# Half of a kernel's intermediate stores moved from the SP queue to the GpSimd queue

## The chip, the core and the metric

The kernel runs on one core of one Trainium2 chip. The metric is the device time of one execution in microseconds (us), and the number for a kernel is the median over several runs. A core has five engines that run side by side: TensorE (PE in the profile; its weight loads are the row PEld), VectorE (DVE), ScalarE (ACT), GpSimd (POOL) and SyncE (SP). Transfers are issued by an engine's instruction stream, in the order in which the instructions stand, and carried out by 16 DMA engines that all streams share.

## The reference

```python
"x": np.random.randn(16, 512, 768), "w1": (768, 3072), "b1": (3072,), "w2": (3072, 768)   # all float32
y = np.matmul(x, w1) + b1
y = 0.5 * y * (1.0 + erf(y / np.sqrt(2.0)))
return np.matmul(y, w2).astype(np.float32)
```

A two-layer perceptron with an exact GELU between the layers: 8192 rows, 768 inputs, 3072 hidden values, 768 outputs.

## The kernel before, in words

Everything is multiplied in fp16 with fp32 sums. Both products go through a bilinear scheme with 20 block products in place of 24: operands are sums and differences of tiles that DVE forms (L341), PE multiplies them, and DVE and ACT combine the partial results from PSUM into the outputs.

**Phase 1** makes g = gelu(x w1 + b1), transposed. The first 512 rows of x are multiplied plainly. The other rows are six blocks, `BLK`: block 0 and block 1 have three pieces of 256 rows each, blocks 2 to 5 three pieces of 512. A block runs through units (three units when pieces have 256 rows, six when they have 512); a unit has 20 products of three or six matmuls (L853) and yields 12 finished tiles of g. For each finished tile, `finish` (L531) adds one ACT instruction with GELU (L537; two for 256-row pieces) that writes a slot of `gst`, a ring of 13 slots of 128 x 512 fp16, and one DMA (L542) that stores the slot, 128 KB, to the tensor `gd` in HBM. A GELU whose slot has not yet been stored must wait. There are 384 such stores: 24 plain ones, 36 in block 0, 36 in block 1 and 72 in each of the blocks 2 to 5.

**Where x comes from.** `x_cast1` (L673) issues from GpSimd a DMA that converts 256 rows of x to fp16 into the tensor `xd` in HBM (L677). `load_x` (L718) issues from SP a transposing DMA from `xd` into one of two x buffers (L728), during the block before the one that uses it. Casts stand one block ahead of the transposes.

**GpSimd's gates.** GpSimd computes nothing in phase 1 after the start. So that a cast does not start too early, `marker` (L377) has DVE write one element after a given product, and `gated` (L368) has GpSimd copy that element (L372) before it issues the DMA. A gated DMA, and all that stands behind it in GpSimd's stream, waits for that copy. In block 4 the gated DMAs are twelve casts of w2 into HBM (L894); in block 5 GpSimd loads w2 and the first g tiles (L934, L988).

**Phase 2** loads g back from `gd`, three 1 MB transfers for each 512 rows (L988), multiplies with w2 (L1026), and stores the outputs from SP (L1049).

**The order** is neither the compiler's nor written out by hand. `Sched` holds tasks with the engines that may run them and planned durations, for example `{"SP": 0.45}` for a store. `S.add` appends a task; `run` (L174) plays the plan forward in model time and emits the task that can start first, with due times for those that prepare later work. PE's tasks keep their written order. So a changed planned duration or engine can also move other tasks in their streams.

Of the kernel before, what the change touches and what calls it, by code (L numbers as in the profile page):

```python
# [252 lines left out]
def kernel(  # L253
# [8 lines left out]
    nc = tc.nc  # L262
# [36 lines left out]
    def a16(off, n):  # L299
        return ar[:, off // 2: off // 2 + n]  # L300
# [4 lines left out]
    S = Sched()  # L305
# [20 lines left out]
    def act_ps(n, src=0):  # L326
        return (n * 0.734 + 267 + src) / 1000
# [33 lines left out]
    def w1_ap(u, w, kt):  # L361

        return a16(O_W1 + (u // 2 * 20 + w) * 2 * W1T + kt * 512 + u % 2 * 256, P)
# [163 lines left out]
    gdone = [[] for _ in range(NU)]  # L527
    stores = []
    gvals = []

    def finish(src, t, row, n, sg, frees):  # L531

        g = Val(gst)
        k = 512 // n
        ft = []
        for y in range(k):
            ft.append(S.add({"ACT": act_ps(n)}, lambda e, y=y: nc.scalar.activation(  # L537
                out=a16(O_GST + g.slot * 1024 + y * n * 2, n), in_=src[1]()[:, y * n:(y + 1) * n], func=ACTF.Gelu,
                bias=b1t[:, t + y:t + y + 1], scale=float(sg)), reads=src[0], frees=frees,
                alloc=g if y == 0 else None, makes=[g], after=ft))  # L540
        un, c0 = row // 512, row % 512
        stores.append(S.add({"SP": 0.45}, lambda e: nc.sync.dma_start(  # L542
            out=gd[un][:, t:t + k, c0:c0 + n], in_=a16(O_GST + g.slot * 1024, 512).rearrange("p (t r) -> p t r", r=n)),
            reads=[g], nbytes=P * 512 * 2, bulk=2))
        gdone[un].append(stores[-1])
        gvals.append(g)
        return ft[-1]
# [117 lines left out]
    BLK = [((512, 768, 1024), 256), ((1280, 7680, 7936), 256)]  # L665
# [68 lines left out]
    def plain_pair(p):  # L734
        for i in range(0, 8, 2):
            qu = [(j // 2, 2 * p + j % 2) if p == 0 else (j % 4, 2 * p + j // 4) for j in (i, i + 1)]
            bv = [Val(bank), Val(bank)]
            for h in range(2):
                for (q, u), b in zip(qu, bv):
                    def mm(e, q=q, u=u, b=b, h=h):  # L740
                        for kc in range(3 * h, 3 * h + 3):
                            nc.tensor.matmul(out=ps[:, b.slot, :],  # L742
                                             lhsT=a16(O_WS[u // 2] + q * 3072 + kc * 512 + u % 2 * 256, P),
                                             rhs=a16(O_XT0 + kc * 1024, 512), start=(kc == 0), stop=(kc == KC - 1),
                                             skip_group_check=True)
                    w = whalf[q][h] if p == 0 else wparts[u][q]
                    t = S.add({"PE": 3 * 0.2158}, mm, reads=[w, x0T], frees=[wsv[u // 2], x0h],
                              **(dict(makes=[b]) if h else dict(alloc=b, makes=[])), after=plain_mm[-1:])
                    if h:
                        plain_mm.append(t)  # L750
            for (q, u), b in zip(qu, bv):
                finish(([b], lambda b=b: ps[:, b.slot, :]), q * 6 + u, 0, 512, 1, [b])
# [3 lines left out]
    def x1_transposes():  # L756
        for s in range(6):
            j, c = divmod(s, 2)
            tr_nat.append(transpose_tile(x1n[s], lambda kc, s=s: a16(O_XN + 6144 + s * 1536 + kc * 256, P),
                                         lambda j=j, c=c: x_third(0, j)[:, :, c * P:(c + 1) * P], xsv[0][j]))  # L760
            xsv[0][3 + j].prods = xsv[0][j].prods
# [30 lines left out]
    def x_sums(b, due0, dur):  # L792

        n = BLK[b][1]
        val = {i: (xsv[b][i], lambda i=i, b=b: xs_ap(b, i)) for i in range(6)}
        outs = {}
        for w, (i, sg) in enumerate(P1_XOUT):
            outs[i] = w
            assert sg == 1
        firstuse = {}  # L800
        for i, (c, w, xx) in enumerate(P1F_ORD):
            firstuse.setdefault(xx, i)
        need = {}
        for (d, op, a, z) in reversed(P1_XOPS):
            need[d] = min(need.get(d, 99), firstuse[outs[d]] if d in outs else 99)
            for q in (a, z):
                need[q] = min(need.get(q, 99), need[d])
        prev = []
        for (d, op, a, z) in sorted(P1_XOPS, key=lambda o: need[o[0]]):
            assert op != "N"  # L810
            va, fa = val[a]
            vb, fb = val[z]
            v = Val({0: sum_first, 1: sum_second, len(BLK) - 1: sum_last}.get(b, sumpool))
            due = due0 + dur * need[d]

            prev = [S.add({"DVE": dve_tt(3 * n)}, lambda e, fa=fa, fb=fb, v=v, op=op: comb(
                e, a16(v.slot, 3 * n), op, fa(), fb()), reads=[va, vb], alloc=v, order=prev, due=due, lock=True)]
            val[d] = (v, lambda v=v: a16(v.slot, 3 * n))
        return [val[i] for (i, sg) in P1_XOUT]
# [8 lines left out]

    def p1_block(b):
        r0, n = BLK[b]  # L830
        dur = 3 * (512 // n) * (n / 2.4 + 2.5) / 1000
        if b:
            xo = x_sums(b, S.pe_ideal, dur)
        last = []
        prods.clear()
        nst = len(stores)
        npair = 512 // n
        for u in range(0, 6, npair):
            if b == 0:
                plain_pair(u // 2)  # L840
                if u == 0:
                    x1_transposes()
                    xo = x_sums(b, S.pe_ideal, dur)
                w1_ops(u // 2, S.pe_ideal - 1.0, ([], w1cast, tr_nat + x0cast)[u // 2], dur)

            ORD, OPS = (P1F_ORD, P1F_OPS) if u == 0 else (P1_ORD, P1_OPS)

            def mm(bk, i, first, lst, u=u, ORD=ORD):
                c, w, xx = ORD[i]
                xa = xo[xx][1]()  # L850
                for kt in range(3):
                    for y in range(npair):
                        nc.tensor.matmul(out=ps[:, bk, y * n:(y + 1) * n],  # L853
                                         lhsT=w1_ap(u + y, w, kt),
                                         rhs=xa[:, kt * n:(kt + 1) * n], start=(first and kt == 0 and y == 0),
                                         stop=(kt == 2), skip_group_check=True)

            def out_final(k, kind, tms, outi, tap, reads, frees, u=u):
                q, j = divmod(outi, 3)
                sg = tms[0][0]  # L860
                return finish((reads, lambda: tap(tms[0])), q * 6 + u, r0[j], n, sg, frees)

            pr = unit(ORD, P1_LEN, OPS, 512, mm, dur, vpool,
                      lambda i: [w1v[u // 2][ORD[i][1]], xo[ORD[i][2]][0]] + (
                          hold + (hold0 if u < 2 else []) if b == len(BLK) - 1 else []), out_final)
            last.extend(pr.values())
            prods.append(list(pr.values()))
            p1_units.extend([list(pr.values())] * npair)
        blk_last[b] = last
        blk_stores[b] = stores[nst:]  # L870
        blk_g[b] = gvals[nst:]
        blk_mid[b] = p1_units[-5]
# [215 lines left out]
```

## Time and profile before

| what | value |
|---|---|
| median of 9 runs | 876.96 us |
| lowest and highest of them | 870.83 and 880.33 us |
| the profiled execution's own time | 877.65 us |
| its span, first to last instruction | 875.9 us |
| mean granted TensorE clock in it | 0.991 |
| busy time in the span | PE 854.6, DVE 653.5, ACT 446.8, POOL 55.8 us |
| median from issue to landing of the 384 g stores (SP) | 3.6 us |
| the same of the 27 x casts (POOL) and the 27 x transposes (SP) | 5.8 and 5.1 us |

The profile is one execution. "Busy" leaves out instructions that only issue a DMA on SP or ACT; a group's idle time is that of the engine just before its instructions, with what ended it. The chain is followed back from the last instruction, at each step to what released it. An event at 349.51 lies 349.51 us after the span's first instruction. The six blocks of phase 1 end near 99, 138, 216, 294, 372 and 454 us.

### The profile page before, as it was taken

The numbers are of one execution on the slowest core, as the hardware profiler recorded it, in microseconds if no ns is written. First come the engines' busy times: TensorE is split into PE (matmuls) and PEld (weight loads), VectorE is DVE, ScalarE is ACT, GpSimd is POOL, SyncE is SP. The second block draws the span as 40 slices with busy tenths as digits, with TensorE's granted clock in tenths as the row PEclk, the third lists the DMA queues.
The fourth block names the chain that finished last, engine by engine and source line by source line (L and its number), as shares of the span: only waits on it lengthen the run. The fifth ranks groups of instructions, "written<-read, shape, count | busy, mean of one in ns | idle before, by whom it ended". The sixth has DMA issues, their size and how long they took to land.

```text
span 875.9 us, 14357 instructions
## 1 busy us (share of the span) xinstructions
PE 854.6 (98%) x4976; PEld 485.9 (55%) x4976; DVE 653.5 (75%) x1103; ACT 446.8 (51%) x810; POOL 55.8 (6%) x117
## 2 busy tenths in 40 slices
PE   7799999999999998999999999999999999999997
PEld 4566885444444443444445666666666666666564
DVE  4879689579668866886799986668766668876763
ACT  5697888777777876687882222222222222222221
POOL 0301011000000111121000000000000000000000
PEclk9899999999999999899999999999999999999999
DMA  9999998976796799786694546665445665444612
GB/s 300 224 203 193 210 207 186 229 205 174 168 234 153 161 228 223 169 257 208 226 317 138 168 151 205 207 216 166 161 153 181 207 217 178 166 158 158 216 64 73
DMA packets 154328, 167.69 MB, mean 191 GB/s; under 512 B 55520, under 2 KB 145632, under 8 KB 147680
## 3 DMA queue, kind: packets, MB, share of 16 engines
q1 hardware_dynamic: 135872, 137.27, 51.6%
q0 software_dynamic: 15296, 29.50, 19.2%
q8 instruction: 39, 0.64, 0.3%
q10 hardware_dynamic: 3088, 0.01, 0.2%
q14 instruction: 33, 0.27, 0.1%
HBM read 99.10 MB, written 90.83 MB: 217 GB/s over the span
## 4 chain that ended last, share of the span: by engine, by line
PE 89%; DMA 4%; DVE 4%; issue 1%; ACT 1%; SPq 0%; DVEq 0%; ACTq 0%
PE ps L1026 46%; PE ps L853 40%; PE ps L742 3%; DMA gd<-ar 3%; DVE vt L341 2%; DVE ar L341 2%; DMA b1t<-in_b_dram 1%; DMA ar<-in_w_dram 1%; ACT ar L537 1%; ACT vt L346 0%; DVE ar L348 0%; PE ps L513 0%; DVE vt L348 0%; DVE ar L519 0%; DVE vt L339 0%
## 5 line engine op out<-in xcount | busy, mean ns | idle before, releaser
L1026 PE MATMUL ps<-ar 128*128 128x384 f16 x2560 | 416.4, 326 | 0.5 <-DVE ar L341 0.5
L853 PE MATMUL ps<-ar 128*128 128x512 f16 (+1 forms) x2160 | 397.2, 347 | 8.6 <-ACT vt L346 4.8
L1026 PEld LDWEIGHTS <-ar 128*128 128x128 f16 x2560 | 250.5, 98 | 166.4 <-issue 0.9
L341 DVE TENSOR_TENSOR ar<-ar 128x1024 f16<-128x1024 f16 (+2 forms) x403 | 277.2, 713 | 70.6 <-DMA ar<-gd 49.3
L853 PEld LDWEIGHTS <-ar 128*128 128x128 f16 x2160 | 213.1, 99 | 192.3 <-issue 13.4
L346 ACT ACTIVATE vt<-ps 128x384 f32<-128x384 f32 (+1 forms) x286 | 148.1, 534 | 290.6 <-PE ps L1026 238.8
L341 DVE TENSOR_TENSOR vt<-ps,vt 128x512 f32<-128x512 f32 (+1 forms) x223 | 141.7, 642 | 97.5 <-ACT vt L346 46.7
L537 ACT ACTIVATE ar<-vt,b1t 128x512 f16<-128x512 f32 (+1 forms) x288 | 176.1, 645 | 43.7 <-DVE vt L341 30.3
L341 DVE TENSOR_TENSOR vt<-vt,ps 128x512 f32<-128x512 f32 (+1 forms) x202 | 131.2, 663 | 11.2 <-PE ps L1026 6.4
L537 ACT ACTIVATE ar<-ps,b1t 128x512 f16<-128x512 f32 (+1 forms) x168 | 96.7, 618 | 7.8 <-PE ps L853 3.3
L346 ACT ACTIVATE ar<-vt 128x384 f32<-128x384 f32 (+1 forms) x33 | 17.6, 532 | 72.2 <-DVE vt L341 72.2
L341 DVE TENSOR_TENSOR vt<-vt 128x384 f32<-128x384 f32 (+1 forms) x65 | 38.6, 594 | 7.9 <-ACT vt L346 5.0
L372 POOL COPY scr<-mkt 1x1 f32<-1x1 f32 x45 | 17.3, 384 | 345.3 <-DVE mkt L382 345.3
L742 PE MATMUL ps<-ar 128*128 128x512 f16 x144 | 31.9, 379 | 2.5 <-DVE ar L348 1.6
L346 ACT ACTIVATE ar<-ar 128x768 f16<-128x768 f16 (+3 forms) x30 | 27.0, 921 | 7.0 <-DMA ar<-in_x_dram 4.2
L341 DVE TENSOR_TENSOR ar<-vt 128x384 f32<-128x384 f32 x49 | 27.3, 557 | 2.9 <-ACT vt L346 1.0
L339 DVE SCALAR_TENSOR_TENSOR vt<-vt,ps 128x512 f32<-128x512 f32 x30 | 20.5, 683 | 6.4 <-PE ps L853 3.9
L742 PEld LDWEIGHTS <-ar 128*128 128x128 f16 x144 | 13.9, 98 | 19.5 <-DVE ar L348 3.5
L339 DVE SCALAR_TENSOR_TENSOR ar<-vt,ps 128x384 f32<-128x384 f32 x31 | 17.2, 555 | 4.9 <-PE ps L1026 1.8
L677 POOL DMA_DIRECT2D xd<-in_x_dram x27 | 13.2, 493 | 2.6 <-issue 2.5
L348 DVE CAST ar<-ar 128x768 f16<-128x768 f32 (+1 forms) x10 | 4.8, 479 | 9.4 <-DMA ar<-in_w_dram 4.9
L341 DVE TENSOR_TENSOR ar<-ps,vt 128x384 f32<-128x384 f32 x15 | 8.4, 557 | 3.8 <-PE ps L1026 3.6
(26 smaller groups left out, 69.3 us busy)
## 6 DMA issues: line engine op xcount, KB each, us to landing
gd<-ar SPq DMA_DIRECT2D x384, 128.0 KB, 3.6
ar<-gd SPq DMA_DIRECT2D x42, 1024.0 KB, 6.2
out_dram<-ar SPq DMA_DIRECT2D x128, 192.0 KB, 3.3
xd<-in_x_dram POOLq DMA_DIRECT2D x27, 384.0 KB, 5.8
ar<-gd POOLq DMA_DIRECT2D x6, 1024.0 KB, 6.5
w2d<-in_w_dram POOLq DMA_DIRECT2D x12, 384.0 KB, 6.7
ar<-w2d POOLq DMA_DIRECT2D x12, 384.0 KB, 5.0
ar<-in_w_dram POOLq DMA_DIRECT2D x8, 384.0 KB, 13.3
```

The source lines that it names most:

```text
L339: eng.scalar_tensor_tensor(out=o, in0=a, scalar=-1.0, in1=b, op0=ALU.mult, op1=ALU.subtract)
L341: eng.tensor_tensor(out=o, in0=a, in1=b, op=ALU.add if op == "+" else ALU.subtract)
L346: nc.scalar.activation(out=o, in_=a, func=ACTF.Copy, scale=float(sg))
L348: eng.tensor_copy(out=o, in_=a)
L372: nc.gpsimd.tensor_copy(out=o[0:1, 0:1], in_=ap[0:1, 0:1])
L537: ft.append(S.add({"ACT": act_ps(n)}, lambda e, y=y: nc.scalar.activation(out=a16(O_GST + g.slot * 1024 + y * n * 2, n), in_=src[1]()[:, y ...
L677: gate, lambda: nc.gpsimd.dma_start(out=xd[a:z, :], in_=xf[a:z, :])),
L742: nc.tensor.matmul(out=ps[:, b.slot, :], lhsT=a16(O_WS[u // 2] + q * 3072 + kc * 512 + u % 2 * 256, P), rhs=a16(O_XT0 + kc * 1024, 512), s ...
L853: nc.tensor.matmul(out=ps[:, bk, y * n:(y + 1) * n], lhsT=w1_ap(u + y, w, kt), rhs=xa[:, kt * n:(kt + 1) * n], start=(first and kt == 0 an ...
L1026: nc.tensor.matmul(out=ps[:, bk, 0:NB], lhsT=xa[:, j, :], rhs=a16(w2v[w][j // 4].slot + j % 4 * NB * 2, NB), start=(first and j == 0), sto ...
```

## The change

The diff lets `finish` choose the issuing engine of a store. While the blocks 1, 2, 3 and 4 are being added, the stores alternate between GpSimd, with a planned 0.7 us, and SP, with a planned 0.45 us as before. In the plain part and in the blocks 0 and 5 all stores stay on SP. No arithmetic, buffer or transfer size changes.

```diff
+    store_eng = [{"SP": 0.45}]
...
-        stores.append(S.add({"SP": 0.45}, lambda e: nc.sync.dma_start(
+        stores.append(S.add(dict(store_eng[len(stores) % len(store_eng)]), lambda e: (nc.sync if e == "SP" else nc.gpsimd).dma_start(
             out=gd[un][:, t:t + k, c0:c0 + n], in_=a16(O_GST + g.slot * 1024, 512).rearrange("p (t r) -> p t r", r=n)),
             reads=[g], nbytes=P * 512 * 2, bulk=2))
...
     def p1_block(b):
         r0, n = BLK[b]
+
+        store_eng[:] = [{"POOL": 0.7}, {"SP": 0.45}] if 0 < b < len(BLK) - 1 else [{"SP": 0.45}]
```

Of the 252 stores of the blocks 1 to 4, 126 go to GpSimd's stream. They stand there between the gates and casts; in the blocks 2 to 4 there are up to seven of them between one gated DMA and the next.

## The prediction

> **What bounds the kernel now.** I began with the page's busy times and costliest groups.
>
> ```profile
> PE 854.6 (98%) x4976; PEld 485.9 (55%) x4976; DVE 653.5 (75%) x1103; ACT 446.8 (51%) x810; POOL 55.8 (6%) x117
> L1026 PE MATMUL ps<-ar 128*128 128x384 f16 x2560 | 416.4, 326 | 0.5 <-DVE ar L341 0.5
> L853 PE MATMUL ps<-ar 128*128 128x512 f16 (+1 forms) x2160 | 397.2, 347 | 8.6 <-ACT vt L346 4.8
> ```
>
> PE is busy 98% of the span. Phase 2 (L1026) has 0.5 us of idle time, and the change does not touch it. Phase 1 (L853) has 8.6 us, of which ACT's copies from PSUM (L346) ended 4.8. Whatever the change can give lies there, with what hangs on it. So next I asked the view of waits what ACT waits for between 99 and 454 us, and the timeline what stands before the largest gap:
>
> ```profile
> ACT ar L537 <- DMA gd<-ar: 5.5, 4, 3.6
> ```
>
> ```profile
> 330.14 4.41 SPq L728 DMA_TRANSPOSE ar<-xd  x1
> ...
> 334.64 2.46 SPq L542 DMA_DIRECT2D gd<-ar  x5
> ...
> 337.19 5.04 SPq L728 DMA_TRANSPOSE ar<-xd  x1
> ...
> 340.13 0.88 POOL L372 COPY scr<-mkt 1x1 f32<-1x1 f32 x1 [4.89 <-DVE mkt L382]
> ...
> 340.95 0.74 POOL L894 DMA_DIRECT2D w2d<-in_w_dram  x1
> ...
> 342.33 9.46 SPq L542 DMA_DIRECT2D gd<-ar  x15
> ...
> 348.25 0.72 ACT L537 ACTIVATE ar<-vt,b1t 128x512 f16<-128x512 f32 x1 [3.60 <-DMA gd<-ar]
> 348.88 1.55 ACT L346 ACTIVATE vt<-ps 128x512 f32<-128x512 f32 x3
> ...
> 349.51 2.72 PE L853 MATMUL ps<-ar 128*128 128x512 f16 x6 [3.43 <-ACT vt L346]
> ```
>
> Read it from the end. PE idles 3.43 us for a PSUM copy of ACT; ACT stands in a GELU that waits 3.60 us for a slot of the store ring; the store that frees it was queued on SP behind a transpose that kept SP's stream for 5.04 us, and 15 stores had piled up behind it. The same at 164.62: an earlier transpose held SP for 6.48 us, two GELUs waited 0.44 and 1.13 us, PE idled 1.12 us. The four waits on stores in the first line are these two places.
>
> Last I asked the table of stretches what the gap does to the clock (columns: us, busy PE, PEld, DVE, ACT, POOL with counts, granted clock, DMA share, GB/s):
>
> ```profile
> 340.00:346.00 6.00, 6.00 (x29) 2.65 (x27) 3.55 (x5) 3.63 (x6) 1.56 (x2) 1.00 1.24 207
> ...
> 349.50:352.00 2.50, 2.49 (x6) 0.84 (x6) 1.37 (x3) 1.54 (x3) 0.91 (x2) 0.50 0.83 276
> 352.00:354.00 2.00, 2.00 (x6) 0.73 (x5) 1.15 (x2) 0.00 (x0) 0.00 (x0) 0.50 0.81 103
> 354.00:356.00 2.00, 2.00 (x7) 0.73 (x6) 1.41 (x3) 0.16 (x1) 0.00 (x0) 0.68 1.17 205
> ```
>
> After the gap PE has half its clock until about 355.3. The time lost to it is 2.5 x 0.5 + 2.0 x 0.5 + 2.0 x 0.32 = 2.9 us, in which PE counts as busy. After the 1.12 us gap the granted clock stayed at 1.00. The two places together cost 3.43 + 2.9 + 1.12 = 7.45 us: the most that the change can bring.
>
> **Part 1: what leaves SP.** 126 of 252 stores, at a median 0.40 us for SP to issue one in the blocks 1 to 4: 50 us of SP's time. What matters is where SP was full. From 317 to 342 a transpose stands every 6.2 to 7.1 us; it holds SP 3.5 to 5.0 us and five stores take 2.46, together 6.0 to 7.5. SP is just over full, and the backlog grows to the 15 stores above. With 2 or 3 stores in each period the sum is 4.5 to 6.5: no lasting backlog even if transposes get no shorter. In the blocks 2 to 4 the first transpose stands behind 3 stores in place of 8. Its readers are the next block's sums and products; no wait of DVE or PE for a transpose is in the list of waits, and block 4's last one lands at 348.0, 24 us before block 5 begins, so a microsecond either way costs nothing.
>
> **Part 2: what GpSimd gets.** The profile has no store from GpSimd; the nearest rows are:
>
> ```profile
> L894 POOL DMA_DIRECT2D w2d<-in_w_dram x12 | 8.9, 739 | 2.8 <-issue 2.8
> L934 POOL DMA_DIRECT2D ar<-w2d x12 | 6.5, 543 | 1.4 <-PE ps L853 1.0 <-ACT ar L537 0.4
> ```
>
> A store has 128 pieces, as L934 has, against 512 for L894. I take 0.54 us, between 0.49 (an x cast) and 0.74: 126 x 0.54 = 68 us over 273 us, beside 28 us that GpSimd is busy there now (3.95 + 7.63 + 6.01 + 7.96 + 2.73 in the table of stretches). In block 4 it is 36 x 0.54 = 19 us of 78. GpSimd is no bound.
>
> One rule speaks against this. The Trainium skill (SBUF — State Buffer, Who interferes with whom) says that VectorE in a two-port mode shuts GpSimd out and so starves the descriptors of a DMA issued from it. The row comes first: the gate's copy (L372) takes 0.17 us alone and up to 0.88 beside DVE's 128x1536 sums, but every x cast in the blocks 1 to 4 takes 0.49, beside such a sum or not. The same section says that a two-input sum has no two-port mode, so on it I would add nothing; read the other way, each store would wait as the gate does, some 0.7 us, which is no wait on PE's path either.
>
> **Part 3: landing.** A GELU reuses a slot 12.0 us (151.36 to 163.36) to 14.3 us (333.94 to 348.25) after the GELU that filled it; a store has that long to land. At the second place the GELU ended at 334.67, its store was issued at 342.33 and landed at 348.17: 7.66 us in SP's queue and 5.84 to land. For a store from GpSimd the ends are 1.7 us (the fastest from SP) and a w2 cast's slowest 7.9 with 0.54 of its own behind it, 8.5. That the issuing engine itself costs little is seen in the same 1 MB g load issued by both:
>
> ```profile
> ar<-gd SPq DMA_DIRECT2D x42, 1024.0 KB, 6.2
> ...
> ar<-gd POOLq DMA_DIRECT2D x6, 1024.0 KB, 6.5
> ```
>
> I take 4 us where no cast is ahead and 8.5 just behind one, plus GELU 0.7 and up to 0.9 for a gate's copy: at most 10.1 us, under 12.0. The SP half lands as its low-backlog stores do, 2 to 6 us after issue.
>
> The Trainium skill (DMA: Bandwidth & Descriptors, Issuing engines are not separate DMA queues) says that spreading issue over engines saves only the sequencer's issue time. Taken alone it would make the gain zero wherever the DMA engines are the limit. Here the issuing stream is what was measured late, 7.66 us of the 13.5 at the second place.
>
> **Part 4: new waits.** A store on GpSimd waits for its GELU; behind it stand the next gate, its cast, and at block 5 the w2 loads. The casts are early: those issued at 137.8, 144.6 and 151.9, the tightest, feed the transposes at 169.8, 177.6 and 182.2, some 24 us after they land. If that cover were gone, each late microsecond would be SP's, and the stores' behind it. Conversely a store waits for a gate that stands before it. Ends: 0 and the longest wait of a gate in block 4, 8.7 us; I take under 1, since the plan orders both by when they can start, and GpSimd has stood idle before nearly every gate so far. At the seam to block 5 one store stands behind the first w2 load; its slot is wanted a ring later: nothing.
>
> **Part 5: moved work.** PE's order is unchanged. On DVE some 35 instructions around block 2's start change places, and one PSUM copy goes from DVE to ACT, 0.6 us, with ACT 58 and DVE 60 of 78 us busy there: 0, with ends -0.6 and +0.6.
>
> **Sum.** 877.65 (span 875.9 and 1.75 around it) - 3.43 - 2.9 = 871.3. Of the 1.12 us at 164.62 I take half, since there the stores also landed late after issue (8.4 to 10.0 us): 870.8. The profiled run is 0.7 above the median, within the spread, so I do not shift it.
>
> **Rivals.** *The stall stays in part* (875.3). The DMA share is 1.24 at 340 to 346, so the DMA engines themselves may be late, and the stores on GpSimd share a queue with the w2 casts. For it: landings of 5 to 7 us in block 4 even after issue. Against: the queue wait was longer than the landing. If 2.5 us of the wait and half the lost clock remain, the gain is 0.9 + 1.45: 877.65 - 2.35 = 875.3.
>
> *Slower: stores caught behind gates* (884). In block 4 the gates stand about 6.6 us apart, and a store queued behind a gate that has not opened waits for PE's progress, while PE waits for the slot. 6.6 + 8.5 + 0.7 = 15.8 us, over the 12.0: a stall of 3.8 us, and with the half clock 6.7. It decides from 12 us between a GELU's start and its store's landing. One such stall replaces the old one; two make 870.8 + 13.4 = 884. For it: GpSimd's stream is strictly in order and has eleven such gates there. Against: the plan puts a store behind a gate only when its GELU ends later.
>
> *The change does not do what it says*: excluded, as 126 stores stand in GpSimd's stream.
>
> **Numbers.** Stalls gone, 0.62; stays in part, 0.20; slower, 0.18. Within 0.5% (872.6 to 881.3) is about what a measurement of this kernel can tell from no change; the three chances fall on either side of it. The floor is 877.65 - 7.45 = 870.2, less 0.6 for Part 5 and 0.6 for spread: 869.0. Above, the second case and the run-to-run spread of the first reach to 877.5, which leaves out most of the third.
>
> **What would show it.** The 3.43 us PE gap and the half clock near 349 gone; L853's idle time near 4 us; GELUs waiting for stores under 1 us in all; SP's run of 15 stores gone; GpSimd's stores at 0.5 to 0.6 us each. Wrong: GELUs waiting for stores issued by GpSimd, gates released while stores stand behind them, a new half-clock stretch, or PE gaps with another releaser.

## The result, and the profile after

The change made the kernel slower. Its median is 882.73 us (17 runs, 876.65 to 898.13), against 875.97 us for the kernel before in the same runs. The ratio is 1.0077, with a 95% interval of 1.0055 to 1.0099. The prediction said 870.8 us, within 869.0 to 877.5. The profiled execution took 882.73 us with a span of 880.8 us, so it stands for the median. The ratios leave out executions over 1.5% above the fastest of their kernel (here 897.65 and 898.13 us); the profiles of only_b4 and b2_casts_late below are such executions, so their gaps may be larger than usual.

The busy times and the costliest groups of the changed kernel come first. (All lines have moved down by one to three: the matmuls L853 are now L856, the GELU is L538, the store L543, the transpose L729.)

```profile
PE 852.0 (97%) x4976; PEld 484.1 (55%) x4976; DVE 650.8 (74%) x1102; ACT 446.9 (51%) x811; POOL 123.3 (14%) x243
L1029 PE MATMUL ps<-ar 128*128 128x384 f16 x2560 | 416.6, 326 | 0.7 <-DVE ar L341 0.5
L856 PE MATMUL ps<-ar 128*128 128x512 f16 (+1 forms) x2160 | 395.2, 346 | 14.7 <-ACT ar L538 5.9
L543 POOL DMA_DIRECT2D gd<-ar x126 | 71.7, 569 | 161.8 <-ACT ar L538 153.4
gd<-ar SPq DMA_DIRECT2D x258, 128.0 KB, 4.3
gd<-ar POOLq DMA_DIRECT2D x126, 128.0 KB, 5.1
```

The moved stores cost GpSimd what was expected, 0.57 us each, and phase 2 is unchanged. But the idle time of phase 1's matmuls rose from 8.6 to 14.7 us, and the largest releaser is new: ACT's GELU, 5.9 us. The stores' median landing rose from 3.6 us to 4.3 on SP and 5.1 on GpSimd. PE's whole idle time (span less busy) rose by 7.5 us, 880.8 - 852.0 against 875.9 - 854.6, and its busy time fell by 2.6: together the 4.9 us by which the span grew.

Next, the view of waits, for ACT between 99 and 454 us, on the same kernel:

```profile
ACT ar L538 <- DMA gd<-ar: 9.4, 3, 3.8
```

The GELUs waited 9.4 us for stores in place of 5.5. The stall at 349 is gone: from 190 us to the end of phase 1's matmuls at 459 PE has no gap over 0.15 us, and SP's run of 15 stores does not occur. The three waits are all at the start of block 2, where before had only its smaller place at 164.62. The timeline shows it (start, duration, engine and line, count, idle time before it and its releaser):

```profile
160.34 3.06 SPq L729 DMA_TRANSPOSE ar<-xd  x1
160.96 0.50 POOL L678 DMA_DIRECT2D xd<-in_x_dram  x1 [0.29 <-issue]
161.48 1.12 POOL L543 DMA_DIRECT2D gd<-ar  x2
...
163.50 1.36 SPq L543 DMA_DIRECT2D gd<-ar  x2
164.97 13.04 SPq L729 DMA_TRANSPOSE ar<-xd  x1
...
177.00 0.72 ACT L538 ACTIVATE ar<-vt,b1t 128x512 f16<-128x512 f32 x1 [3.67 <-DMA gd<-ar]
...
178.10 2.03 SPq L543 DMA_DIRECT2D gd<-ar  x3
181.52 1.84 ACT L538 ACTIVATE ar<-ps,b1t 128x512 f16<-128x512 f32 x3 [3.80 <-DMA gd<-ar]
182.25 6.33 PE L856 MATMUL ps<-ar 128*128 128x512 f16 x21 [5.88 <-ACT ar L538]
...
185.94 1.33 ACT L538 ACTIVATE ar<-vt,b1t 128x512 f16<-128x512 f32 x2 [1.97 <-DMA gd<-ar]
```

From 161.48 until SP's next transpose at 164.97, stores go out promptly on both streams: GpSimd issues its two in 1.12 us. They then do not land. The store that GpSimd issued at 161.48 landed at 176.91, after 15.4 us, and released the GELU at 177.00. The store that SP issued at 163.50 landed at 181.44, after 17.9 us, and released the GELU at 181.52. The transpose at 160.34 landed after 20.75 us, and the next one held SP's stream for 13.04 us. So in these two waits, behind which PE stood, neither stream is what is late: the transfers of both are. Only the third wait, 1.97 us at 185.94, is for a store that SP issued late, at 178.10, behind that transpose.

The table of stretches shows what the DMA engines did meanwhile (us, busy PE, PEld, DVE, ACT, POOL with counts, granted clock, DMA share, GB/s), first of the kernel before, then of the changed kernel:

```profile
160.00:176.00 16.00, 14.88 (x70) 6.66 (x68) 8.84 (x15) 11.67 (x20) 0.66 (x2) 1.00 1.12 230
```

```profile
160.00:176.00 16.00, 16.00 (x76) 7.23 (x75) 9.03 (x17) 10.23 (x17) 4.63 (x10) 1.00 1.07 125
176.00:182.00 6.00, 0.38 (x2) 0.10 (x1) 1.15 (x2) 1.20 (x2) 0.56 (x1) 0.73 1.25 176
182.00:186.00 4.00, 3.75 (x10) 1.36 (x10) 1.38 (x2) 2.03 (x5) 1.08 (x2) 0.55 1.19 218
```

From 160 to 176 us the DMA share (the time that packets took, summed, against 16 engines) is 1.07, about as before, but the engines moved only 125 GB/s in place of 230. The granted clock is half again, from 178.78, within the gap, to 185.61; of that PE was busy for 3.36 us (from 182.25), so some 1.7 us are lost.

The DMA queues in this stretch (queue, packets, MB, share of 16 engines; then issues, KB each, median us to landing), first of the kernel before:

```profile
q1 hardware_dynamic: 6573, 2.88, 83.2%
q0 software_dynamic: 51, 0.79, 28.0%
```

and of the changed kernel:

```profile
q1 hardware_dynamic: 1968, 0.69, 56.2%
q0 software_dynamic: 256, 1.29, 50.3%
...
xd<-in_x_dram POOLq DMA_DIRECT2D x2, 384.0 KB, 13.5
gd<-ar POOLq DMA_DIRECT2D x6, 128.0 KB, 15.3
gd<-ar SPq DMA_DIRECT2D x2, 128.0 KB, 17.9
ar<-xd SPq DMA_TRANSPOSE x2, 20.6
```

q1 carries what SP issues, q0 what GpSimd issues. Before, SP's queue had most of the engines' time and moved 2.88 MB. After, the two queues share the time about evenly and SP's moves 0.69 MB. Everything in flight is late at once.

One part of the profiled difference is chance: a PE gap of 4.68 us at 87.11, in block 0, ahead of the first moved store. A second profile of the changed kernel has none there, and a second one of the kernel before has one of 2.21 us at 84.14.

### The profile page after: what moved, and what is told of

Same layout as the page of the kernel before. It is cut to its first block, busy times and chain, and to the rows that moved or that the text cites. A ratio compares the mean times of both kernels' runs of the same rounds, so it can differ in the third digit from the quotient of the medians.

```text
span 880.8 us, 14358 instructions
## 1 busy us (share of the span) xinstructions
PE 852.0 (97%) x4976; PEld 484.1 (55%) x4976; DVE 650.8 (74%) x1102; ACT 446.9 (51%) x811; POOL 123.3 (14%) x243
## 2 busy tenths in 40 slices
DMA packets 139929, 167.69 MB, mean 190 GB/s; under 512 B 55521, under 2 KB 127201, under 8 KB 133281
## 4 chain that ended last, share of the span: by engine, by line
PE 86%; DMA 6%; DVE 4%; issue 1%; ACT 1%; SPq 0%; DVEq 0%; ACTq 0%
PE ps L1029 43%; PE ps L856 40%; DMA gd<-ar 3%; DVE ar L341 2%; PE ps L743 2%; DVE vt L341 2%; DMA b1t<-in_b_dram 1%; ACT ar L538 1%; DMA ar<-gd 1%; DMA ar<-in_w_dram 1%; ACT vt L346 0%; DVE ar L519 0%; SPq L729 0%; DVE ar L348 0%; SPq L543 0%
## 5 line engine op out<-in xcount | busy, mean ns | idle before, releaser
L856 PE MATMUL ps<-ar 128*128 128x512 f16 (+1 forms) x2160 | 395.2, 346 | 14.7 <-ACT ar L538 5.9
L856 PEld LDWEIGHTS <-ar 128*128 128x128 f16 x2160 | 212.1, 98 | 197.5 <-issue 18.1
L538 ACT ACTIVATE ar<-vt,b1t 128x512 f16<-128x512 f32 (+1 forms) x288 | 176.2, 645 | 43.7 <-DVE vt L341 29.3
L341 DVE TENSOR_TENSOR vt<-vt,ps 128x512 f32<-128x512 f32 (+1 forms) x202 | 131.2, 663 | 17.2 <-PE ps L856 10.4
L538 ACT ACTIVATE ar<-ps,b1t 128x512 f16<-128x512 f32 (+1 forms) x168 | 96.6, 618 | 16.1 <-DMA gd<-ar 11.3
L543 POOL DMA_DIRECT2D gd<-ar x126 | 71.7, 569 | 161.8 <-ACT ar L538 153.4
L372 POOL COPY scr<-mkt 1x1 f32<-1x1 f32 x45 | 12.8, 283 | 120.5 <-DVE mkt L382 120.4
L743 PEld LDWEIGHTS <-ar 128*128 128x128 f16 x144 | 13.8, 98 | 20.9 <-DVE ar L348 5.2
L678 POOL DMA_DIRECT2D xd<-in_x_dram x27 | 13.7, 511 | 3.4 <-issue 3.2
```

The costliest lines, as they stand in the source:

```text
L341: eng.tensor_tensor(out=o, in0=a, in1=b, op=ALU.add if op == "+" else ALU.subtract)
L372: nc.gpsimd.tensor_copy(out=o[0:1, 0:1], in_=ap[0:1, 0:1])
L543: stores.append(S.add(dict(store_eng[len(stores) % len(store_eng)]), lambda e: (nc.sync if e == "SP" else nc.gpsimd).dma_start(out=gd[un][ ...
L678: gate, lambda: nc.gpsimd.dma_start(out=xd[a:z, :], in_=xf[a:z, :])),
L743: nc.tensor.matmul(out=ps[:, b.slot, :], lhsT=a16(O_WS[u // 2] + q * 3072 + kc * 512 + u % 2 * 256, P), rhs=a16(O_XT0 + kc * 1024, 512), s ...
L856: nc.tensor.matmul(out=ps[:, bk, y * n:(y + 1) * n], lhsT=w1_ap(u + y, w, kt), rhs=xa[:, kt * n:(kt + 1) * n], start=(first and kt == 0 an ...
```

## The experiments

Five theories stood against each other. **A**: only the jam at block 2's start costs; elsewhere the change helps. **B**: a second queue makes the transposes slower in every block. **C**: transposes, converting casts and the stores of a second queue, in flight together, slow each other several-fold. **D**: the stores of a second queue do it by themselves, with or without casts. **E**: GpSimd's stream, in order with its gates, holds the stores back.

In the readings below "landing" is from a transpose's issue to its landing. Block 2 is the stretch 138 to 216 us, its start the part up to about 190 us in which its six transposes stand, and block 4 is 294 to 372 us.

**All but block 2** (skip_b2). The stores of block 2 stay on SP.

```diff
-        store_eng[:] = [{"POOL": 0.7}, {"SP": 0.45}] if 0 < b < len(BLK) - 1 else [{"SP": 0.45}]
+        store_eng[:] = [{"POOL": 0.7}, {"SP": 0.45}] if b in (1, 3, 4) else [{"SP": 0.45}]
```

> Stores alternate between GpSimd and SP in the blocks 1, 3 and 4; block 2 keeps all stores on SP. Theory A (the loss is one jam at the start of block 2, where three x casts, the x transposes and the stores of two queues meet; elsewhere the change only helps): the 5.9 us PE gap near 182 is gone, the 3.4 us gap of before near 349 too, and the time is 870 to 873, a ratio to before of 0.992 to 0.998. Theory B (a second queue of stores slows the transposes and so the stores in every block alike): the transposes of blocks 3 and 4 still take 8 to 9 us to land against 5 to 7 before, and the time is 878 to 882, ratio 1.003 to 1.008.

Measured: 879.89 us (12 runs), ratio 1.0058 [1.0024, 1.0093]. The timeline of PE in the changed block 4, and at block 2's start where nothing is changed:

```profile
172.37 4.69 PE L856 MATMUL ps<-ar 128*128 128x512 f16 x21 [1.05 <-ACT ar L538]
180.80 153.36 PE L856 MATMUL ps<-ar 128*128 128x512 f16 x702 [3.73 <-ACT vt L346]
335.62 4.04 PE L856 MATMUL ps<-ar 128*128 128x512 f16 x18 [1.46 <-ACT ar L538]
343.72 110.50 PE L856 MATMUL ps<-ar 128*128 128x512 f16 x502 [4.05 <-ACT vt L346]
```

Theory A falls. Block 2 on SP alone still stalls 4.8 us, and block 4 with both queues stalls 5.5 us; the transposes of block 4 land at a median of 12.4 us. Most of the loss is still there, so it does not all come from the alternation in block 2.

**Block 2 alone** (only_b2).

```diff
+        store_eng[:] = [{"POOL": 0.7}, {"SP": 0.45}] if b == 2 else [{"SP": 0.45}]
```

> Stores alternate in block 2 alone; all other stores are on SP as before. Theory A: the jam at block 2's start is there (transposes or casts that take over 12 us to land, a PE gap over 3 us near 165 to 185 and a half-clock stretch behind it), and block 4's gap stays as before: 882 to 885, ratio 1.006 to 1.011. Theory B: a quarter to a third of the loss, 877 to 879, ratio 1.001 to 1.004.

Measured: 878.11 us (12 runs), ratio 1.0040 [1.0007, 1.0073]. The timeline at block 2's start:

```profile
160.62 12.65 SPq L729 DMA_TRANSPOSE ar<-xd  x1
...
177.43 6.47 PE L856 MATMUL ps<-ar 128*128 128x512 f16 x21 [5.42 <-ACT ar L538]
```

It is the jam of the full change, with a transpose that holds SP for 12.65 us and a gap of 5.42 us. So the jam needs no alternation in the blocks around it.

**Block 4 alone** (only_b4), the block whose stall the prediction wanted removed.

```diff
+        store_eng[:] = [{"POOL": 0.7}, {"SP": 0.45}] if b == 4 else [{"SP": 0.45}]
```

> Stores alternate in block 4 alone. Theory A: the 3.4 us gap near 349 and its half clock are gone, and nothing is added: 869.5 to 872.5, ratio 0.992 to 0.997. Theory B: what the shorter SP backlog gives is taken by slower landings: 875 to 879, ratio 0.999 to 1.004.

Measured: 880.27 us (12 runs), ratio 1.0042 [1.0003, 1.0081]. The removal did not come: PE has gaps of 1.16 us at 336.02 and 5.12 us at 345.19, and transposes in block 4 land at a median of 12.2 us and at most after 18.2. The profiled execution took 886.01 us. In the full change SP and GpSimd have the same order of instructions in block 4, and there is no gap.

**The changed kernel once more** (after_again), no edit.

> The changed kernel once more, for a second profile. Theory A: again a PE gap of several us near 160 to 190 with transposes that take over 12 us to land; the 4.7 us gap near 87 of the first profile, which lies ahead of the first moved store, is chance and may be missing. Theory B: the transposes of blocks 2 to 4 take 8 us or more to land on average, and gaps stand in any block. If the gap near 87 is there again, it belongs to the change and both theories lack it.

Measured: 883.28 us. Gaps of 6.07 us at 176.73 and 3.97 at 187.16, the first behind a transpose that held SP for 12.14 us; none near 87, none in block 4. The jam at block 2's start is there in both profiles; the gap in block 0 is not.

**Casts away, stores on both queues** (casts_late_alt). On the changed kernel, the casts of the blocks 2 to 4 are gated into their units 3 to 5, when the transposes are over; three casts that stood at block 2's start are made in block 1. The transposes, stores and amounts stay.

```diff
-              1: [prods[1][12], prods[2][3], prods[2][12]]}.get(b, [p[10] for p in prods])
-        if b == 2:
-            for r, t in zip(x_rows(3)[3:], (prods[0][3], prods[0][12], prods[1][3])):
-                x_cast1(*r, gate=marker(t), order=poolq)
+              1: [prods[1][2], prods[1][9], prods[1][16], prods[2][3], prods[2][10], prods[2][17]]}.get(
+                  b, [prods[j][i] for j in range(3, len(prods)) for i in (3, 13)])
...
-                g = marker(prods[k // 2][(3, 13)[k % 2]])
+                g = marker(prods[3 + k // 4][(3, 8, 13, 18)[k % 4]])
```

> The changed kernel with the casts moved off the transposes: in the blocks 2, 3 and 4 GpSimd's casts are gated into the units 3 to 5, after the x transposes of the block, and the three x casts that stood at the start of block 2 go into block 1. Theory C (a transpose, a cast and the stores of a second queue in flight together slow each other several times over): transposes of blocks 2 to 4 land in 7 us or less on average, no PE gap over 1 us between 150 and 350, 868 to 874 us. Theory D (stores on a second queue slow the transposes by themselves): transposes still take 8 us or more, 877 to 883 us.

Measured: 872.65 us (10 runs), ratio 0.9967 [0.9939, 0.9995]. Transposes of the blocks 2, 3 and 4 land at medians of 4.5, 4.6 and 5.1 us, none after more than 6.8; PE has no gap over 1 us from 99 to 454. With both queues but without casts beside the transposes of these blocks there is no jam: theory D falls, and C stands.

**Casts away, stores on SP** (casts_late_sp): the same edit on the kernel before.

> The same move of the casts, but with all stores on SP as in the kernel before. Both theories: the transposes of blocks 2 to 4 land faster than before (under 6 us on average), the gaps near 164 and 349 shrink, 868 to 873 us. If it is 874 or more, casts beside transposes were not what delays the stores in the kernel before.

Measured: 880.18 us (10 runs), ratio 1.0053 [1.0022, 1.0083], outside what was expected. In the blocks 2 to 4 it did as expected: landings at medians of 4.1, 4.0 and 3.9 us, no stall from 140 to 397. But the timeline of PE shows where the six casts now stand, in block 1:

```profile
135.00 0.82 PE L853 MATMUL ps<-ar 128*128 128x256 f16 x6 [3.39 <-ACT vt L346]
...
137.23 12.82 PE L853 MATMUL ps<-ar 128*128 128x256 f16 x66 [1.41 <-DVE vt L339]
```

Six casts in the three units of block 1 stand beside that block's transposes, one of which took 13.8 us to land, and made a new stall there. The view of waits, for ACT from 99 to 140 us:

```profile
ACT ar L537 <- DMA gd<-ar: 8.0, 3, 5.6
```

So this kernel does not measure what moving casts away is worth, and I repeated it without touching block 1 (below). It does show that casts beside transposes stall a kernel whose stores are all on one queue, too.

The pair shows one thing more. casts_late_alt has the same six casts in block 1, with half of the stores on GpSimd. There the transposes of block 1 land at a median of 5.4 us and after 10.4 at most, no GELU waits for a store, and the kernel takes 872.65 us against 880.18. With these casts the second queue gained 0.9%, where with the casts in their old places it lost 0.8%. In the kernel on SP alone a transpose in block 1 held SP for 6.22 us and stores stood behind it: that is the kind of loss that the prediction hoped to win back. So theory C does not hold wherever the three kinds meet, and why it does not in block 1 is not shown.

**Both queues only when the transposes are over** (late_units). Alternation in the units 4 and 5 of the blocks 2 to 4, so 36 stores on GpSimd; the casts stay as in the kernel before.

```diff
+            store_eng[:] = [{"POOL": 0.7}, {"SP": 0.45}] if b in (2, 3, 4) and u >= 4 else [{"SP": 0.45}]
```

> Stores alternate in the units 4 and 5 of the blocks 2, 3 and 4 alone (36 stores on GpSimd), where no transposes are in flight but casts and gates are. Theories C and D: no loss, 873 to 877 us, ratio 0.998 to 1.002, and stores from GpSimd land in 3 to 6 us. Theory E (GpSimd's strict order, with gates and casts ahead of stores, makes stores late): about a third of the change's loss, 877 to 879 us, and GELUs wait for stores in these units.

Measured: 876.22 us (10 runs), ratio 1.0014 [0.9979, 1.0049]; no difference. The view of the store's line, from 138 to 372 us (duration min/median/max; then who waited for it, us and times; then landing):

```profile
L543 POOL DMA_DIRECT2D gd<-ar x36: 539/540/595, 190.3 to 369.5; - x36
...
  ACT ar L538: 0.4, 1
...
DMA to landing us min/median/max: 1.7/3.9/8.7
```

These stores pass the same gates in the same stream, and GELUs waited 0.4 us for all the stores of that line. So theory E falls by these waits; the time alone, with an interval that has both forecasts in it, would not decide. In the jam of the changed kernel, too, GpSimd's stores were issued at once, but for one that waited 2.7 us for older transfers to land.

**ACT's queue in place of GpSimd's** (act_ring).

```diff
-        ... (nc.sync if e == "SP" else nc.gpsimd).dma_start(
+        ... (nc.sync if e == "SP" else nc.scalar).dma_start(
...
-        store_eng[:] = [{"POOL": 0.7}, {"SP": 0.45}] if 0 < b < len(BLK) - 1 else [{"SP": 0.45}]
+        store_eng[:] = [{"ACT": 0.45}, {"SP": 0.45}] if 0 < b < len(BLK) - 1 else [{"SP": 0.45}]
```

> The alternation of the change with ACT's queue in place of GpSimd's, casts where they were. If a second queue beside the transposes is what hurts (theory D), transposes of blocks 2 to 4 land in 8 us or more and there is a gap of several us near 160 to 190: 880 us or more. If it takes GpSimd's own queue, in which stores and casts share packets (theory C in its narrow form), transposes land in 5 to 7 us and the time is 871 to 878 us, with up to some us added by ACT's own issue time.

Measured: 894.73 us in one execution. The view of the transposes' line at block 2's start (issue time min/median/max, first and last start; then landing):

```profile
L729 SPq DMA_TRANSPOSE ar<-xd x6: 1390/1882/9551, 154.1 to 191.9; - x6
DMA to landing us min/median/max: 4.5/7.3/15.8
```

There is a stall without a single store from GpSimd, with a PE gap of 6.16 us at 181.81. By itself it says little: the kernel before has one as large in its second profile (below). The blocks 3 and 4 say more. There the transposes land at medians of 8.1 and 9.5 us, as in the changed kernel (8.2 and 8.5) and not as in the kernel before (4.4 and 6.8). So, in one profile, another queue beside the casts is enough to slow the transposes; GpSimd's way of issuing is not needed. What makes this kernel slower still is in the view of waits:

```profile
ACT ar L538 <- DMA ar<-xd: 9.7, 1, 9.7
```

A GELU reads nothing from a transpose. ACT stood for 9.7 us until a transpose landed, and the instruction that it then ran ahead of the GELU is the issue of a store, at 179.94: the store held the engine that has the GELUs to do. The trace's semaphore numbers tell why. A transfer signals its landing through a semaphore; in this program SP and ACT take turns with the same eight, and before one is used again the issuing engine waits until its earlier transfer has landed. The store at 179.94 had the number of the transpose that SP issued at 164.09, which landed at 179.86. So this wait comes from how the program's semaphores are shared, not from ACT's queue.

**Casts away, block 1 untouched** (late234_sp on the kernel before, late234_alt on the changed one). As casts_late, but the casts of block 1 and the three at block 2's start keep their places.

```diff
-              1: [prods[1][12], prods[2][3], prods[2][12]]}.get(b, [p[10] for p in prods])
+              1: [prods[1][12], prods[2][3], prods[2][12]]}.get(
+                  b, [prods[j][i] for j in range(3, len(prods)) for i in (3, 13)])
...
-                g = marker(prods[k // 2][(3, 13)[k % 2]])
+                g = marker(prods[3 + k // 4][(3, 8, 13, 18)[k % 4]])
```

> All stores on SP as before; in the blocks 2, 3 and 4 the casts for the block after next and the w2 casts are gated into the units 3 to 5, behind the block's transposes; the x casts of block 1 and the three at the start of block 2 stay where they were. Theory C: transposes of the blocks 3 and 4 land in about 4 us, as in casts_late_sp, and without its six casts in block 1 there is no stall near 135; a part of the stall near 164 may stay: 868 to 873 us, ratio 0.990 to 0.997. If the stalls of the kernel before do not come from casts beside transposes: 874 to 877 us.

> The same move of the casts with the changed kernel's alternating stores. Theory C: in the blocks 3 and 4 transposes land in about 5 us, and only the start of block 2, where two or three casts still meet transposes and both queues' stores, can stall: 870 to 877 us, at or a little above the same kernel with all stores on SP. Theory D: 878 us or more.

Measured: late234_sp 871.72 us (12 runs), ratio 0.9953 [0.9926, 0.9980]; late234_alt 871.12 us (12 runs), ratio 0.9950 [0.9924, 0.9976]. Both beat both kernels, and they do not differ from each other. The groups of PE from 99 to 454 us in late234_alt:

```profile
L856 PE MATMUL ps<-ar 128*128 128x512 f16 (+1 forms) x1761 | 346.9, 360 | 0.5 <-ACT vt L346 0.4
```

In the changed kernel the idle time of this group is 6.7 us in the same window; here it is 0.5. In late234_sp it is 1.8. The medians of the transposes' landing, each pair for the blocks 3 and 4:

| transposes to landing, us | casts beside them | casts in units 3 to 5 |
|---|---|---|
| stores on SP | 4.4 / 6.8 (before) | 3.9 / 3.9 (late234_sp) |
| stores on both queues | 8.2 / 8.5 (after) | 4.8 / 5.2 (late234_alt) |

Theory B is right in direction: a second queue costs some 1 us of landing without casts. It is the second queue and the casts together that bring it to 8 us.

**The kernel before once more** (before_again), no edit.

> The kernel before once more, for a second profile. If its stalls are one fixed plan, the gaps of 1.1 us near 164 and 3.4 us near 349 with the half clock come again; if they are chance meetings of transfers, their sizes and places in the blocks 0, 2 and 4 differ. Transposes of blocks 2 to 4 land in 5 to 7 us on average either way.

Measured: 878.45 us. The timeline of PE:

```profile
175.44 1.23 PE L853 MATMUL ps<-ar 128*128 128x512 f16 x3 [3.42 <-ACT ar L537]
...
197.22 2.97 PE L853 MATMUL ps<-ar 128*128 128x512 f16 x13 [1.56 <-ACT vt L346]
```

There is no gap near 349, and 6.2 us of idle time in block 2 where the first profile had 1.4. The kernel before has no fixed stall in block 4: where its transposes meet the casts badly differs from one execution to the next.

**Only block 2's casts away** (b2_casts_late). The changed kernel, with the six casts of block 2 that serve block 4 gated into the units 3 to 5; nothing else.

```diff
-              1: [prods[1][12], prods[2][3], prods[2][12]]}.get(b, [p[10] for p in prods])
+              1: [prods[1][12], prods[2][3], prods[2][12]],
+              2: [prods[j][i] for j in range(3, len(prods)) for i in (3, 13)]}.get(b, [p[10] for p in prods])
```

> The changed kernel with one thing moved: the six x casts that are issued during block 2 for block 4's data are gated into block 2's units 3 to 5, behind its transposes. Casts of the other blocks stay. Theory C, with the loss in block 2: the gap of about 6 us between 160 and 190 is gone, transposes of block 2 land in 5 to 7 us on average in place of 11.7, those of the blocks 3 and 4 still take 8 to 9; the jam cost 5.9 + 0.4 us of idle PE and some 1.7 us of half clock in the changed kernel's profile, so 873 to 877 us, ratio 0.997 to 1.002. If the loss lies in the slower transposes of the blocks 3 and 4 instead: 879 to 882 us, ratio 1.005 to 1.008.

Measured: 876.29 us (12 runs), ratio 0.9987 [0.9950, 1.0024]. Against 1.0077 that is 0.9% of 876, some 8 us, and the kernel is level with before again. The view of the transposes' line at block 2's start, first of the changed kernel, then of this one:

```profile
L729 SPq DMA_TRANSPOSE ar<-xd x6: 1974/2745/13037, 150.1 to 190.3; - x6
...
DMA to landing us min/median/max: 5.9/8.6/20.7
```

```profile
L729 SPq DMA_TRANSPOSE ar<-xd x6: 1428/1592/2321, 151.6 to 180.5; - x6
...
DMA to landing us min/median/max: 4.4/5.7/7.3
```

And the timeline of PE in this kernel:

```profile
143.98 189.29 PE L856 MATMUL ps<-ar 128*128 128x512 f16 x876 [0.25 <-ACT vt L346]
...
343.22 29.05 PE L856 MATMUL ps<-ar 128*128 128x512 f16 x127 [3.90 <-ACT vt L346]
```

The jam at block 2's start is gone by moving six casts, with all 126 stores left on GpSimd. SP's and ACT's instructions keep their order; on DVE the marks for the gates move with the casts, and two sums change places, near 92 and 215 us. In block 4, where the casts still stand beside the transposes (landings at a median of 12.4 us), a stall stands now (the profiled execution took 884.14 us).

## Why the prediction was wrong

**The step that failed is Part 3, the landing.** It took 4 us for a store from GpSimd, 8.5 behind a cast, and 2 to 6 us for one from SP. In the jam, for the stores issued from 161.48 to 169.79, both queues took 13.7 to 17.9 us, over the 12.0 us that a slot allows, and PE stood. Each row that the term came from was right for its own traffic: one queue with small packets and now and then a cast. The sum of them is not the price of all three together. A row that warned of it was in the profile before. The prediction laid PE's gap at 164.62 to a transpose that held SP for 6.48 us:

```profile
156.35 6.48 SPq L728 DMA_TRANSPOSE ar<-xd  x1
...
163.36 0.72 ACT L537 ACTIVATE ar<-vt,b1t 128x512 f16<-128x512 f32 x1 [1.13 <-DMA gd<-ar]
```

But the store that this GELU waited for had been issued at 153.28, ahead of that transpose, and landed at 163.28, 10.0 us later, with three casts and two transposes beside it. That place, the same where the jam now stands, was late in landing, not in issuing. The prediction names the 8.4 to 10.0 us in its sum, yet Part 3 ends at 8.5 for GpSimd and at 6 for SP. In block 2 of late234_alt, with six of its casts moved behind the transposes, both queues' stores land in 1.7 to 6.0 us, so the term was not wrong in general, but in the stretch that decides.

**Part 1** held for the issuing stream alone: SP's run of 15 is gone. It also said that there is no lasting backlog "even if transposes get no shorter". They got longer, from a median of 1.50 to 2.75 us of issue at block 2's start and 13.04 at most, and SP's half of the stores queued behind that one.

**Part 2** held: 0.54 us at the median for a store on GpSimd. The rule that VectorE starves GpSimd's descriptors was rightly not added: the longest of the 33 stores found from 138 to 216 us took 0.72 us.

**Part 4** held: the view of the store's line from 138 to 216 us has GpSimd idle for GELUs, 38.8 us, not for gates; one store waited 2.7 us for older transfers to land. The cover of the casts was not used up.

**The sum** subtracted 6.3 us of a stall in block 4 as if it were fixed. The second profile of the kernel before does not have it, but stalls 6.2 us elsewhere. What is fixed is that transposes and casts meet in each block; which meeting becomes a stall differs. In block 2, five profiles with the stores of that block's first units on SP and the casts in place have 0.0, 1.4, 4.1, 4.8 and 6.2 us of idle PE (late_units, before, only_b4, skip_b2, before_again), three with both queues 6.0, 6.5 and 10.0 (only_b2, after, after_again). So the change does not create the jam; it makes a small or middling one large, in these few profiles, whose ranges overlap at 6.0 to 6.2 us. The means are 3.3 and 7.5 us, and the half clock comes on top. Nor is the loss in block 2 alone. Over the blocks 2 to 4 PE's idle time is 4.8 and 6.2 us in the two profiles of the kernel before, 6.5 and 10.0 in those of the changed kernel, and 10.3 in skip_b2 and 10.5 in only_b4, where half or more of it stands in block 4.

**The rivals.** "The stall stays in part" named the right mechanism, the DMA engines being late by themselves, but with the wrong place and a gain of 2.35 us. The slower rival came out near the measured time (884 us) by a mechanism that did not occur: no store that a GELU waited for stood behind a gate. Its deciding point, 12 us from a GELU's start to its store's landing, was right, and its price of a stall (6.7 us with the clock) near what the jam cost: 6.3 us of idle PE and 1.7 of half clock. That the time came close is luck: it had put the wait behind a gate in GpSimd's stream.

The Trainium skill (DMA: Bandwidth & Descriptors, Issuing engines are not separate DMA queues) was weighed and put aside for the 7.66 us in SP's queue. It says that all engines' transfers run on the same 16 DMA engines and interleave there, whoever starts them, so that spreading them saves the sequencer's issue time only. That was the part of it that counted here: late234_sp and late234_alt, 0.9953 and 0.9950, show that once the casts are out of the way the second queue gains nothing that can be measured. The pair casts_late_sp and casts_late_alt shows the other part: where a transpose held SP's stream in block 1, the second queue was worth 0.9%.

**What stays open.** Why the engines move only 125 GB/s in the jam is not shown. The packets of the transposes lasted a mean of 69 ns each from 160 to 182 us, against 25 ns in the kernel before from 150 to 172, and the casts' packets of 24 KB 2.8 us against 2.3. The same page of the Trainium skill (Queues, rings and completion order) says that a DMA engine takes turns between the queues that have work, a packet at a time. That would let GpSimd's large packets, of casts and of stores, take half of the engines' time from SP's packets of 256 bytes, as the shares 56.2 and 50.3% look; no run here separates that from another cause, nor shows whether the page's packets are those of the profile. In act_ring, where GpSimd's queue carries the casts alone, it still has 51.8% of the engines from 160 to 176 us, so GpSimd's stores are not needed for that. The second queue also let more be in flight: SP and GpSimd each have eight semaphores to signal landings, and from 138 to 372 us at most 8 transfers of SP and 3 of GpSimd are in flight at once in the kernel before, 8 and 8 in the changed one. act_ring speaks against this as the whole cause, with at most 6 of SP, 4 of ACT and 3 of GpSimd, but no run varies it by itself. Nor is it shown why block 4 stalls in skip_b2, only_b4 and b2_casts_late, but in neither profile of the full change; in skip_b2 and only_b4 SP and GpSimd have the full change's order of instructions there.

## What to carry to other kernels

Before a transfer is moved to another queue, ask whether the old stream was late in issuing or the transfers late in landing, and look for the stretch where all kinds of traffic are in flight at once: its landings, not those of quiet stretches, are the term to use, and the quiet rows of the old kernel do not bound them from above. When transposes jam, move what meets them: here 24 casts gated into the later half of their blocks gave 0.5%, whichever queue took the stores; where they go matters, as with three more of them in block 1 the kernel on SP alone was 0.5% slower than before. And a stall seen in one profile is one draw: a second profile of the same kernel tells whether there is a fixed loss to win back.

## What the runs showed of the hardware

- A transposing DMA of 256 rows holds the issuing stream 1.4 us when little else is in flight (late234_sp, 1.40 to 1.42 us in block 4) and up to 13.04 us when much is. What stands behind it in that stream waits.
- A DMA share above 1 says nothing of throughput: 1.12 with 230 GB/s and 1.07 with 125 GB/s, in the same stretch of the two kernels.
- A completion semaphore that SP and ACT share ties their streams together: ACT was held 9.7 us ahead of a store until a transpose of SP had landed (act_ring).
- In the blocks 2 to 5 the same 128 KB store goes in 1024-byte packets from SP (512 in block 1), and in 4096-byte packets from GpSimd. The page's count of DMA packets fell from 154328 to 139929 for the same 167.69 MB.
